# Casts and subtractions of the up projection's left forms, put in program order on their engines

## The chip, the core and the metric

One Trainium2 chip, of which the program uses one core. The metric is the device time of one execution in microseconds (us). The kernel before was run three times: 2421.71, 2421.89 and 2420.68 us, median 2421.71. All engine names are those of the profile: PE multiplies matrices, DVE, ACT and POOL work on vectors, SP issues most of the transfers.

## The reference

The program is one layer of a hybrid trunk on 1024 positions of width 1024 (three token mixers, cross-attention, a gated MLP). Only the MLP matters here. Its first half is a projection to 2 x 2816 columns, a causal convolution of width 3 over the positions, a SiLU and a product:

```
h = rms_norm(x, norm_ffn_g)
u, v = split(h @ ffn_w_up, 2)              # D_FF = 2816 each
y = silu(causal_conv3(u, ffn_conv_w, ffn_conv_b)) * v
x = x + y @ ffn_w_down
```

Everything is float32. A float32 product is made on PE from three products of rounded operands (type fp32r): an operand x is split into hi, a cast of x, and lo, the difference x - hi, and hi·hi, hi·lo and lo·hi are added up in PSUM.

## The kernel before

The up projection is `ffn_up`. It walks over 22 pairs f = 0 to 21. A pair holds 128 columns of u and 128 of v, and is done for all 1024 positions as a 2 x 2 block product with seven block products instead of eight. The right operands (T1 to T4, B11, B21, B22; 512 positions each, with hi and lo) are made once, at the end of `trunk`. The left operands, called forms here, are made afresh in every pair by the generator `left` (L1294 to L1317): A11, A12 and A22 are parts of the weights as loaded (tile `raw`), S1 to S4 are sums and differences of such parts, made on POOL (L1308). For each form `left` then issues two instructions:

- the cast (L1315) on ACT, from the part or sum into the first half of a tile `wf`,
- the subtraction (L1316) into the second half, on DVE for odd and on POOL for even numbers of a running count of forms.

`prod` (L1318 to L1324) multiplies a form with its right operand in 12 matmuls (L1323), three to each of four slices: hi·hi and hi·lo, which need the cast alone, and lo·hi, which needs the subtraction too. Where PE has done the first two matmuls of a form and not yet the third, it has started on a form whose subtraction is not there.

The tiles `wf` come from a pool with two tags of two buffers each, and the count of forms picks the tag. So the form made now takes the buffer of the form made four forms earlier, and its cast has to wait until the product of that form is done.

Pairs 0 to 5 have five forms, in program order S2, S3, S1, A22, S4: their products with B11 and B21 are done ahead of time (`ahead`, while the trunk ends) and stored. Pairs 6 to 21 have seven: A11, S2, S3, S1, A12, A22, S4. With seven forms to a pair, A11 of a pair takes the buffer of S1 of the pair before.

The products of one pair go to three places in PSUM: `ps_a` (A11 with B11, then A12 with B21), `ps_b2` (S2 with T2) and one tile of two banks, `ps_cd` (S3 with T3, S1 with T1, A22 with T4, S4 with B22). DVE reads them in turn: u2 (L1384), u3 (L1386), the upper half of vt (L1388), the lower half (L1393), the upper half of u (L1395); ACT copies `ps_a` to s1 (L1348) and u (L1391). A22 may write `ps_cd` only when vt (L1388) has been read, because waits go by whole tiles. Then y is made: L1397 (ACT), L1398 and L1399 (DVE), the SiLU L1400 (ACT), and the product with vt, L1401 (DVE).

No order is written out by hand in this function. The program is issued under a scheduler with a model of the engines' times, and that scheduler picks for every engine which of the ready instructions comes next; the streams of two or three pairs are therefore mixed on each engine. After the last pair comes `ffn_down`, whose loads of weights (tile `wdr`, L1452), sums of them (L1459, DVE) and casts (L1466, ACT) are mixed into the last pairs in the same way.

Of the kernel before, what the change touches and what calls it, by code (L numbers as in the profile page):

```python
# [12 lines left out]
F32 = mybir.dt.float32  # L13
# [4 lines left out]
ALU = mybir.AluOpType  # L18
# [78 lines left out]
class K:  # L97
# [1197 lines left out]
    def left(self, r1, r2, which, sp):  # L1295

        nc = self.nc
        V, A, G = nc.vector, nc.scalar, nc.gpsimd
        q = {f"A{n}{k + 1}": r[:, 4 * k:4 * k + 4, :] for n, r in ((1, r1), (2, r2)) if r is not None for k in range(2)}
        sums = {"S1": ("A21", "A22", ALU.add), "S2": ("S1", "A11", ALU.subtract), "S3": ("A11", "A21", ALU.subtract),  # L1300
                "S4": ("A12", "S2", ALU.subtract)}

        def get(n):
            if n not in q:
                a, b, op = sums[n]
                a, b = get(a), get(b)
                q[n] = sp.tile([P, 4, P], F32, tag=n, name=n, bufs=2 if n in ("S1", "S2") else 1)
                G.tensor_tensor(out=q[n], in0=a, in1=b, op=op)  # L1308
            return q[n]

        for n in which:
            x = get(n)
            self.nform = getattr(self, "nform", 0) + 1
            f = self.wp.tile([P, 2, 4, P], F32R, tag=("whi", "wlo")[self.nform % 2], name="wf")
            A.copy(out=f[:, 0], in_=x)  # L1315
            (V if self.nform % 2 else G).tensor_tensor(out=f[:, 1], in0=x, in1=f[:, 0].bitcast(F32), op=ALU.subtract)  # L1316
            yield f  # L1317

    def prod(self, ps, f, x, start, stop):
        n = 0  # L1320
        for k in range(4):
            for a, b in ((0, 0), (0, 1), (1, 0)):
                self.nc.tensor.matmul(ps, lhsT=f[:, a, k, :], rhs=x[b][:, k, :], start=(start and n == 0), stop=(stop and n == 11),  # L1323
                                      skip_group_check=not start)  # L1324
                n += 1
# [305 lines left out]
```

## Time and profile before

| | |
|---|---|
| median of three runs | 2421.71 us |
| the profiled execution, its own time | 2418.76 us |
| span of that execution in the profile | 2417.0 us |
| PE busy | 2312.8 us, 96% of the span |
| DVE, ACT, POOL busy | 1373.9, 908.9, 695.2 us |

The span is the time between the first and the last instruction of the profile; the execution's own time is 1.76 us longer. The times in rows are counted from the span's start. A row of the timeline has the start, the duration, the engine, the line, the operation, what it writes and reads, how many there are, and in brackets how long the engine stood idle before it and what it waited for. Matmuls overlap each other, so the pace of PE is read from one start to the next and not from the duration of one.

In the profile the up projection's end of the trunk lies at about 1728 to 1778 us, its pairs from there to about 2185 us, and the down projection behind.

### The profile page before, as it was taken

To read this page: it belongs to the slowest core of one execution; us is meant where nothing else is said; L and a number is where in the kernel's file an instruction comes from. 1 tells how busy PE (TensorE), PEld (TensorE's weight loads), DVE (VectorE), ACT (ScalarE), POOL (GpSimd) and SP (SyncE) were. 2 spreads that over 40 slices of the span, in tenths; PEclk is the share of its full clock that TensorE was granted. 3 is DMA by queue.
4 is the path that set the end of the run, shared out by engine and by line. 5 is a ranking of instruction groups with operands and counts; after the bars stand their busy time and mean duration, and the time that the engine had idled before them with its cause. 6 is when DMAs were issued, how large, how long until landed. Compare 5 with 4: busy or idle time off the path is not lost. (4 is left out here: it accounts for less than half of the span.)

```text
span 2417.0 us, 34889 instructions
## 1 busy us (share of the span) xinstructions
PE 2312.8 (96%) x13988; PEld 1887.5 (78%) x13988; DVE 1373.9 (57%) x2098; ACT 908.9 (38%) x1430; POOL 695.2 (29%) x580
## 2 busy tenths in 40 slices
PE   7999999899999999999999999999898999998998
PEld 7877768686778787888878778888676888886886
DVE  6446374757424557454564464545547656667775
ACT  6542213131314435344442233443333333334443
POOL 1011001010111333333132440141456666551041
PEclk9999999999999999999999999999999999999999
DMA  8653312121222111111103662224243322238333
GB/s 302 221 176 125 92 58 97 58 92 45 76 70 81 53 53 37 35 60 54 44 27 121 215 213 96 96 88 135 106 165 135 111 94 105 105 142 306 97 96 122
DMA packets 110930, 266.14 MB, mean 110 GB/s; under 512 B 27248, under 2 KB 31984, under 8 KB 110768
## 3 DMA queue, kind: packets, MB, share of 16 engines
q1 hardware_dynamic: 108656, 258.25, 31.9%
q0 software_dynamic: 1248, 4.46, 0.5%
q8 instruction: 110, 1.80, 0.3%
q10 hardware_dynamic: 864, 1.20, 0.1%
q14 instruction: 52, 0.43, 0.1%
HBM read 194.40 MB, written 69.47 MB: 109 GB/s over the span
## 5 line engine op out<-in xcount | busy, mean ns | idle before, releaser
L155 PE MATMUL ps_d<-hThi,whi 128*128 128x512 f32 x1056 | 425.9, 404 | 2.0 <-DVE Ktt L261 1.6
L157 PE MATMUL ps_d<-hTlo,whi 128*128 128x512 f32 x1056 | 424.2, 402 | 0.0
L159 PE MATMUL ps_d<-hThi,wlo 128*128 128x512 f32 x1056 | 424.1, 402 | 0.0
L140 ACT CAST whi<-raw 128x1024 fp32r<-128x1024 f32 (+1 forms) x170 | 167.2, 989 | 331.4 <-PE ps_d L157 155.4
L143 DVE TENSOR_TENSOR wlo<-raw,whi 128x1024 fp32r<-128x1024 f32 (+1 forms) x125 | 156.9, 1262 | 138.2 <-ACT whi L140 138.2
L155 PEld LDWEIGHTS ps_d<-hThi,whi 128*128 128x128 f32 x1056 | 199.9, 189 | 44.5 <-issue 3.2
L157 PEld LDWEIGHTS ps_d<-hTlo,whi 128*128 128x128 f32 x1056 | 199.9, 189 | 42.8 <-issue 4.6
L159 PEld LDWEIGHTS ps_d<-hThi,wlo 128*128 128x128 f32 x1056 | 199.7, 189 | 42.7 <-issue 4.2
L143 POOL TENSOR_TENSOR wlo<-raw,whi 128x1024 fp32r<-128x1024 f32 (+1 forms) x45 | 96.8, 2150 | 433.1 <-ACT whi L140 388.4
L1490 PE MATMUL ps_dn<-wd,ap 128*128 128x512 f32 x924 | 213.2, 393 | 7.1 <-ACT wd L1466 6.7
L1490 PEld LDWEIGHTS ps_dn<-wd,ap 128*128 128x128 f32 x924 | 175.1, 190 | 45.2 <-ACT wd L1466 7.1
L1315 ACT CAST wf<-S 128x512 fp32r<-128x512 f32 x88 | 54.7, 622 | 165.0 <-PE ps_cd L1323 76.5
L1466 ACT CAST ap<-acr 128x512 fp32r<-128x512 f32 x77 | 47.9, 623 | 104.2 <-PE ps_dn L1490 93.2
L1467 DVE TENSOR_TENSOR ap<-acr,ap 128x512 fp32r<-128x512 f32 x77 | 61.4, 799 | 41.4 <-ACT ap L1466 40.6
L745 DVE CUSTOM_DVE_ANT_0 a_p<-ps_s,a_bias 128x512 f32<-128x512 f32 (+3 forms) x96 | 51.7, 553 | 50.3 <-PE ps_s L743 45.0
L159 PE MATMUL ps_d<-ohi,wlo 128*128 128x512 f32 x192 | 75.9, 395 | 3.3 <-DVE wlo L143 3.3
L1316 POOL TENSOR_TENSOR wf<-S,wf 128x512 fp32r<-128x512 f32 x44 | 62.0, 1409 | 56.1 <-ACT wf L1315 56.1
L755 ACT ACTIVATE a_p<-a_p,a_nm 128x128 f32<-128x128 f32 (+7 forms) x64 | 49.2, 770 | 75.2 <-POOL a_nm L751 57.8
L157 PE MATMUL ps_d<-olo,whi 128*128 128x512 f32 x192 | 75.8, 395 | 0.0
L155 PE MATMUL ps_d<-ohi,whi 128*128 128x512 f32 x192 | 75.8, 395 | 0.0
L1113 POOL TENSOR_SCALAR ms<-ms 128x1 f32<-128x1 f32 x30 | 11.1, 371 | 224.0 <-ACT xn L1112 146.1
L1308 POOL TENSOR_TENSOR S<-raw 128x512 f32<-128x512 f32 x44 | 58.9, 1341 | 35.6 <-DVE wf L1316 21.8
(436 smaller groups left out, 5386.3 us busy)
## 6 DMA issues: line engine op xcount, KB each, us to landing
raw<-t_in SPq DMA_DIRECT2D x66, 512.0 KB, 3.6
raw<-t_up SPq DMA_DIRECT2D x50, 512.0 KB, 3.5
th_dram<-th SPq DMA_DIRECT2D x24, 512.0 KB, 2.8
mth<-th_dram SPq DMA_DIRECT2D x24, 512.0 KB, 3.7
wdr<-ffn_w_down SPq DMA_DIRECT2D x44, 256.0 KB, 5.2
acr<-act_dram SPq DMA_DIRECT2D x44, 256.0 KB, 2.7
act_dram<-y SPq DMA_DIRECT2D x20, 512.0 KB, 2.6
acr<-sums_dram SPq DMA_DIRECT2D x33, 256.0 KB, 2.6
```

The costliest lines, as they stand in the source:

```text
L140: nc.scalar.copy(out=hi, in_=raw)
L143: eng.tensor_tensor(out=lo, in0=raw, in1=hi.bitcast(F32), op=ALU.subtract)
L155: nc.tensor.matmul(o, lhsT=hi[:, k, :], rhs=xhi(k, h), start=(k == 0), stop=False)
L157: nc.tensor.matmul(o, lhsT=hi[:, k, :], rhs=xlo(k, h), start=False, stop=False)
L159: nc.tensor.matmul(o, lhsT=lo[:, k, :], rhs=xhi(k, h), start=False, stop=(k == nk - 1))
L745: V.tensor_tensor_reduce(out=p_[:, a:b], in0=ps[:, 0:b - a], in1=bias[:, 1024 - n + a:1024 - n + b], op0=ALU.add, op1=ALU.max, scale=1.0, ...
L755: A.activation(out=pr[c][:, 0:n], in_=pr[c][:, 0:n], func=AF.Exp, bias=nm[:, c:c + 1], accum_out=Z[:, c:c + 1])
L1308: G.tensor_tensor(out=q[n], in0=a, in1=b, op=op)
L1315: A.copy(out=f[:, 0], in_=x)
L1316: (V if self.nform % 2 else G).tensor_tensor(out=f[:, 1], in0=x, in1=f[:, 0].bitcast(F32), op=ALU.subtract)
L1467: V.tensor_tensor(out=t[:, 1], in0=z, in1=t[:, 0].bitcast(F32), op=ALU.subtract)
L1490: T.matmul(ps[t], lhsT=a[:, p, P * t:P * t + P], rhs=w[:, q, :], start=(not behind and j == 0 and n == 0), stop=(j == NJ - 1 and n == 2), ...
```

## The change

Each of the two instructions of a form is now issued through a helper, `inorder`. The helper keeps, for a key, the last instruction that was issued with it, and tells the scheduler that the next one of the same key has to stand behind it. There are three keys: all casts (ACT), the subtractions on DVE, and the subtractions on POOL. The sums (L1308) have none. What is computed, the buffers, the transfers and the number of instructions stay the same.

```
             f = self.wp.tile([P, 2, 4, P], F32R, tag=("whi", "wlo")[self.nform % 2], name="wf")
-            A.copy(out=f[:, 0], in_=x)
-            (V if self.nform % 2 else G).tensor_tensor(out=f[:, 1], in0=x, in1=f[:, 0].bitcast(F32), op=ALU.subtract)
+            e = self.nform % 2
+            self.inorder("A", lambda: A.copy(out=f[:, 0], in_=x))
+            self.inorder(e, lambda: (G, V)[e].tensor_tensor(out=f[:, 1], in0=x, in1=f[:, 0].bitcast(F32), op=ALU.subtract))
             yield f
+
+    def inorder(self, n, f):
+
+        last = self.__dict__.setdefault("kinds", {})
+        with self.tc.issue_after(last[n].ins) if n in last else ExitStack():
+            last[n] = f()
```

In the changed kernel the cast is L1316 and the subtraction L1317, and every later line has a number that is 7 higher (the matmul is L1330).

The scheduler's answer to the new rule shows in the order of the instructions. First ACT, from the cast of pair 8's S4 (`wf_15678`) to that of pair 9's A12 (`wf_15783`). `raw_15563` is pair 9's weight tile, `S2_15731`, `S1_15729` and `S3_15749` its sums. Before:

```order
L1315 CAST wf_15678<-S4_15676 128x512
L1315 CAST wf_15733<-S2_15731 128x512
L1400 ACTIVATE y_15547<-y_15547 128x1024
L1391 COPY u_14365<-ps_a_15567 128x512
L1315 CAST wf_15707<-raw_15563 128x512
L1315 CAST wf_15767<-S1_15729 128x512
L1315 CAST wf_15751<-S3_15749 128x512
L1348 COPY s1_15722<-ps_a_15706 128x512
L1315 CAST wf_15783<-raw_15563 128x512
```

With the change:

```order
L1316 CAST wf_15678<-S4_15676 128x512
L1407 ACTIVATE y_15547<-y_15547 128x1024
L1398 COPY u_14365<-ps_a_15567 128x512
L1316 CAST wf_15707<-raw_15563 128x512
L1316 CAST wf_15733<-S2_15731 128x512
L1316 CAST wf_15751<-S3_15749 128x512
L1355 COPY s1_15722<-ps_a_15706 128x512
L1316 CAST wf_15767<-S1_15729 128x512
L1316 CAST wf_15783<-raw_15563 128x512
```

The cast of S2 (`wf_15733`), which stood two places ahead of that of A11 (`wf_15707`), now stands behind it, and that of S1 behind that of S3.

Second PE, at the end of pair 8's product of S1 with T1 (`wf_15628`, the buffer that A11 of pair 9, `wf_15707`, takes over). Before:

```order
L1323 MATMUL ps_cd_15587<-T1lo_14151,wf_15628 128x512
L1323 MATMUL ps_cd_15587<-T1hi_14150,wf_15628 128x512
L1323 MATMUL ps_b2_15725<-T2hi_14141,wf_15733 128x512
L1323 MATMUL ps_b2_15725<-T2lo_14142,wf_15733 128x512
L1323 MATMUL ps_b2_15725<-T2hi_14141,wf_15733 128x512 x2
...
L1323 MATMUL ps_a_15706<-B11hi_13794,wf_15707 128x512
L1323 MATMUL ps_a_15706<-B11lo_13795,wf_15707 128x512
L1323 MATMUL ps_cd_15587<-T4hi_14159,wf_15660 128x512
```

With the change:

```order
L1330 MATMUL ps_cd_15587<-T1lo_14151,wf_15628 128x512
L1330 MATMUL ps_cd_15587<-T1hi_14150,wf_15628 128x512
L1330 MATMUL ps_a_15706<-B11hi_13794,wf_15707 128x512
L1330 MATMUL ps_a_15706<-B11lo_13795,wf_15707 128x512
L1330 MATMUL ps_b2_15725<-T2hi_14141,wf_15733 128x512
L1330 MATMUL ps_b2_15725<-T2lo_14142,wf_15733 128x512
L1330 MATMUL ps_cd_15587<-T4hi_14159,wf_15660 128x512
```

The twelve matmuls of pair 9's S2 (`ps_b2_15725`) stood between the end of S1 and the start of A11; now A11 follows S1 directly, and of S2 two matmuls come next and ten after A22 (`wf_15660`) and A11. At the next change of pairs S2's twelve all come after A22.

Third PE, at the change from pair 0 to pair 1. `wf_14655` is S1 and `wf_14671` A22 of pair 0; `wf_14729` is S2 and `wf_14747` S3 of pair 1. Before:

```order
L1323 MATMUL ps_cd_14614<-T1hi_14150,wf_14655 128x512
L1323 MATMUL ps_b2_14721<-T2hi_14141,wf_14729 128x512
L1323 MATMUL ps_b2_14721<-T2lo_14142,wf_14729 128x512
L1323 MATMUL ps_cd_14722<-T3hi_14291,wf_14747 128x512
L1323 MATMUL ps_cd_14722<-T3lo_14292,wf_14747 128x512
L1323 MATMUL ps_cd_14614<-T4hi_14159,wf_14671 128x512
```

With the change:

```order
L1330 MATMUL ps_cd_14614<-T1hi_14150,wf_14655 128x512
L1330 MATMUL ps_cd_14614<-T4hi_14159,wf_14671 128x512
L1330 MATMUL ps_cd_14614<-T4lo_14160,wf_14671 128x512
...
L1330 MATMUL ps_cd_14614<-T4hi_14159,wf_14671 128x512
L1330 MATMUL ps_b2_14721<-T2hi_14141,wf_14729 128x512
L1330 MATMUL ps_b2_14721<-T2lo_14142,wf_14729 128x512
```

The twelve matmuls of A22 of pair 0 moved ahead of the first matmuls of pair 1.

## Rows read from the trace of the kernel before

**Rows 1.** The page: busy us, share of the span and instructions of each engine.
```profile
PE 2312.8 (96%) x13988; PEld 1887.5 (78%) x13988; DVE 1373.9 (57%) x2098; ACT 908.9 (38%) x1430; POOL 695.2 (29%) x580
```
**Rows 2.** Windows: stretch, us; busy (instructions) of PE, PEld, DVE, ACT, POOL; clock; DMA; GB/s.
```profile
1777.90:1805.50 27.60, 21.84 (x85) 16.61 (x85) 12.74 (x16) 8.97 (x12) 18.46 (x14) 0.94 0.37 123
1805.50:1864.00 58.50, 51.98 (x216) 39.62 (x216) 38.97 (x39) 17.72 (x24) 42.77 (x29) 1.00 0.40 136
1907.83:1946.10 38.27, 38.27 (x168) 31.45 (x168) 23.93 (x26) 14.93 (x23) 24.25 (x17) 1.00 0.30 104
2156.90:2192.20 35.30, 25.03 (x108) 19.56 (x107) 23.93 (x31) 12.03 (x18) 9.34 (x8) 0.94 0.97 363
```
**Rows 3.** Timeline of PE and ACT at a change of pairs (pair 9 to 10).
```profile
1945.36 0.39 PE L1323 MATMUL ps_cd<-T1hi,wf 128*128 128x512 f32 x1
1945.58 0.39 PE L1323 MATMUL ps_b<-T2hi,wf 128*128 128x512 f32 x1
1945.78 0.62 ACT L1315 CAST wf<-raw 128x512 fp32r<-128x512 f32 x1 [0.56 <-PE ps_cd L1323]
...
1948.52 0.39 PE L1323 MATMUL ps_a<-B11hi,wf 128*128 128x512 f32 x1
```
**Rows 4.** Timeline of PE and ACT at two changes of pairs between pairs 2 and 5.
```profile
1820.90 0.39 PE L1323 MATMUL ps_cd<-T1hi,wf 128*128 128x512 f32 x1
1821.32 0.62 ACT L1315 CAST wf<-S 128x512 fp32r<-128x512 f32 x1 [1.08 <-PE ps_cd L1323]
1821.99 0.50 PE L1323 MATMUL ps_cd<-T3hi,wf 128*128 128x512 f32 x1 [0.71 <-ACT wf L1315]
1822.33 0.40 PE L1323 MATMUL ps_cd<-T3lo,wf 128*128 128x512 f32 x1
...
1837.34 0.39 PE L1323 MATMUL ps_cd<-T1hi,wf 128*128 128x512 f32 x1
1838.49 0.50 PE L1323 MATMUL ps_cd<-T3hi,wf 128*128 128x512 f32 x1 [0.76 <-ACT wf L1315]
```
**Rows 5.** PE's waits from 1805.5 to 1864 us: us in total, times, longest.
```profile
PE ps_cd L1323 <- ACT wf L1315: 3.1, 4, 0.9
```
**Rows 6.** Timeline of the end of the trunk: ACT and PE, forms made ahead.
```profile
1738.10 0.62 ACT L1315 CAST wf<-raw 128x512 fp32r<-128x512 f32 x1 [3.38 <-PE ps_a L1323]
1738.63 0.58 ACT L1257 CAST T1hi<-ps_T 128x512 fp32r<-128x512 f32 x1
1739.99 0.33 PE L1254 MATMUL ps_T<-ident,t 128*128 128x128 f32 x1 [1.09 <-DVE T1lo L1258]
```
**Rows 7.** Timeline of the change from pair 0 to pair 1: ACT, PE, DVE.
```profile
1772.74 0.63 ACT L1315 CAST wf<-raw 128x512 fp32r<-128x512 f32 x1
...
1782.68 0.39 PE L1323 MATMUL ps_cd<-T1hi,wf 128*128 128x512 f32 x1
...
1783.11 0.69 DVE L1388 TENSOR_TENSOR vt<-ps_cd,u 128x512 f32<-128x512 f32 x1 [3.19 <-PE ps_cd L1323]
...
1785.01 0.58 PE L1323 MATMUL ps_b<-T2hi,wf 128*128 128x512 f32 x1 [1.94 <-ACT wf L1315]
```
**Rows 8.** Timeline of the hand-over to the down projection: DVE and PE.
```profile
2169.14 0.69 DVE L1459 TENSOR_TENSOR wdr<-wdr 128x512 f32<-128x512 f32 x1 [5.85 <-DMA wdr<-ffn_w_down]
...
2178.59 0.47 PE L1323 MATMUL ps_cd<-T4hi,wf 128*128 128x512 f32 x1 [2.69 <-DVE vt L1388]
...
2182.45 0.47 PE L1323 MATMUL ps_cd<-B22hi,wf 128*128 128x512 f32 x1 [0.87 <-DVE vt L1393]
...
2192.14 1.22 PE L1490 MATMUL ps_dn<-wd,ap 128*128 128x512 f32 x2 [6.70 <-ACT wd L1466]
```
**Rows 9.** Timeline of DVE and POOL at the changes from pair 8 to 9 and 9 to 10.
```profile
1926.36 1.21 DVE L1401 TENSOR_TENSOR y<-y,vt 128x1024 f32<-128x1024 f32 x1
...
1944.77 1.29 POOL L1316 TENSOR_TENSOR wf<-S,wf 128x512 fp32r<-128x512 f32 x1
1944.79 2.35 DVE L1401 TENSOR_TENSOR y<-y,vt 128x1024 f32<-128x1024 f32 x1 [1.13 <-ACT y L1400]
...
1947.06 0.68 DVE L1388 TENSOR_TENSOR vt<-ps_cd,u 128x512 f32<-128x512 f32 x1
```

## The prediction

> **What bounds the kernel now.** I read the page's busy times first: PE is busy for 96% of the span, the other engines for less than 60% [rows 1]. So a change of order can cost or bring time only where PE stands still or runs at a slow clock, and the next view is the windows, by stage [rows 2]. Over two whole pairs of the steady part (7 forms each), PE is busy in 38.27 of 38.27 us: 168 matmuls, 0.228 us each, at a granted clock of 1.00, the 2.4 GHz level. Nothing can be won there; it can only be lost. PE stands idle for 5.8 us in the first two pairs (27.60 - 21.84), for 6.5 us in pairs 2 to 5 (58.50 - 51.98), and for 10.3 us at the hand-over to the down projection (35.30 - 25.03). These are all that an order of casts could win.
>
> The timeline then tells why the steady part has no gaps [rows 3]. The last matmul of pair 9's S1 starts at 1945.36. The cast of A11 of pair 10 needs the buffer that S1 frees, and starts 0.42 us later, at 1945.78. It hurts nobody, because PE goes on with S2 of pair 10 at 1945.58 and comes to A11 only at 1948.52: the twelve matmuls of S2 are the cover of this cast, and they take 2.94 us where twelve at 0.228 take 2.73.
>
> **The change, part by part.** No instruction, transfer or buffer is added or taken away. What counts is which order on PE follows from the order of the casts.
>
> *The cover at the change of pairs.* By the order of the changed kernel, PE goes from S1 of a pair straight to A11 of the next, whose cast cannot start before S1's product is done; S2's cast now stands behind A11's on ACT, so there is no other form to go on with. This holds at the changes from 7 to 8 up to 20 to 21: 14 places (at 6 to 7, A22 still lies between). The steady part has no such gap to measure, but pairs 2 to 5 have: there a cast of S3 waits in the same way for the product of S1 [rows 4]. In the first of the two the last matmul starts at 1820.90, the cast at 1821.32 (0.42 us later, as in rows 3), and the next matmul at 1821.99: 1.09 us from start to start instead of 0.228, so 0.86 us lost, and the second matmul follows after 0.34 instead of 0.228, 0.11 more: 0.97. In the second it is 1837.34 to 1838.49, 1.15, so 0.92 + 0.11 = 1.03 us. I take 0.98. That one cast is waited for and not two is because the cast of S2 starts right behind A11's and is done within the first two matmuls of A11. What the new order gives back is the 2.94 - 2.73 = 0.2 us by which S2 is stretched in every other pair, since its third matmul now comes after A22: 0.1 per change. 14 x (0.98 - 0.1) = **+12.3 us**. Bounds: 14 x 0.71 = +9.9 (the shorter idle time by itself) and 14 x 1.03 = +14.4.
>
> *The forms made ahead.* The cast at 1738.10 that stands in front of that of T1hi at 1738.63 [rows 6] is moved behind it. At most 0.53 us of PE's wait of 1.09 us for T1lo goes with that; other casts could come to stand there instead. I take **-0.3 us**, bounds -0.5 and +0.5.
>
> *Pairs 0 and 1.* After S1 of pair 0 PE waits 1.94 us for the cast of S2 of pair 1 [rows 7]. Now A22 of pair 0 is first; its cast was done at 1773.4 already. A22 must wait until DVE has read `ps_cd`: that reading starts at 1783.11 and takes 0.69, so PE goes on at about 1783.85 instead of 1785.01: -1.2 us, and S2's cast is ready when A22 is through. The load of the next raw weights is held a little longer, so I take **-1.0 us**. Low bound: -1.94, and all that the clock withholds in this stretch (granted 0.94 of 27.60 us, 1.66 us [rows 2]), together -3.6. High bound: the wait for the reading, 1783.85 - 1782.68 - 0.228 = 0.9 us, comes on top of the old one: +0.9.
>
> *Pairs 2 to 5.* PE's order stands as it was; the four waits for a cast [rows 5] stay. **0**; if POOL's sums of pairs 3 and 5, whose order differs, come late, one more wait of 0.76 in each [rows 4]: +1.5, the high bound; nothing there is made earlier, so the low bound is 0.
>
> *The hand-over.* PE's waits here are for vt (2.69 and 0.87) and for the first cast of the down projection's weights (6.70), and DVE stands 5.85 us for a load of these weights, with the work of pairs 20 and 21 behind it [rows 8]. In the new order SP has that load further back, and DVE the first of the sums behind pair 21's u3, while three more of them now stand in front of the work that PE waits for. These cancel about, by the durations (0.69 each against 5.85 that were mostly hidden behind PE's own work): **+0.5 us**. Bounds: all 10.3 us gone, or one more wait of 2.69 us.
>
> **Sum:** 12.3 - 0.3 - 1.0 + 0 + 0.5 = +11.5 us. The profiled execution took 2418.76 us, so 2430.3 on its basis. It lies 2.95 us below the median of the three runs (2421.71); on the median's basis the prediction is **2433.2 us**, 0.47% more than before. A measurement of this kernel can tell about 0.2%, 4.8 us, from no change.
>
> **The rivals.**
>
> *The hand-over pays for the gaps (not slower).* DVE's 5.85 us on the load of weights is the one large stall whose place in the order is changed. If u, u2 and vt of the last pairs, freed from it, bring the down projection's first sums and casts forward, up to 10.3 us of idle PE come back. Without the hand-over the sum is +11.0, so this decides from the point where more than 11.0 - 4.8 = 6.2 us are won; in full the sum is 11.0 - 10.3 = +0.7, 2422.4 us. For it: the load is what that stall waits for, by its row. Against it: PE's last wait, 6.70 us, is for weights that arrive while DMA is at 0.97 [rows 2], so they come no earlier by another order of DVE; the loads begin later in the new order rather than earlier. 0.14; in 0.04 of it the gaps are also smaller than priced and the kernel gets faster by over 0.2%.
>
> *A22 waits too (slower still).* In every other pair the product L1401 on DVE takes 2.35 us instead of 1.21, beside a subtraction on POOL, and vt (L1388) stands behind it: it ends at 1947.74, 2.38 us after the last S1 matmul's start [rows 9, 3]. S2's cover of 2.94 us hid that. After the change A22 comes 1.15 + 0.34 + 0.23 = 1.7 us after that start at these changes, so it would wait another 0.7 us: 7 x 0.7 = +4.9, 2438.1 us. Against it: the subtraction on POOL that lies beside L1401 is that of S2, and it moves behind A11's cast, past the end of L1401. 0.08. The Trainium skill ("SBUF — State Buffer", section "SBUF: two separate sides") calls the port pair that DVE and POOL share an exclusive lock, where whoever comes second is blocked for the whole instruction; the trace agrees (2.35 against 1.21, with 1.29 of POOL beside it), and by that rule the lengthening goes with POOL's subtraction.
>
> *The clock falls at the gaps (much slower).* After the wait of 1.94 us in pair 0 to 1 the clock was lower for a time: 0.94 over that window, 1.66 us lost. If each of the 14 new gaps had that effect, 14 x 1.66 = +23 us, 2456 us. Against it: pairs 2 to 5 have gaps of 0.7 to 0.9 us and the granted clock there is 1.00 [rows 2, 5]; those gaps are no closer together than one pair. 0.04. The Trainium skill ("TensorE: Matmul & The Clock Gate", section "A second HAM failure mode: psum-queue depth-cycling") says that frequent short idle times between groups of matmuls can make the clock go up and down, with the time of a single matmul looking right; it would make this rival's case, and the rows of pairs 2 to 5 do not bear it out.
>
> That the order does not come about at all is not a case: the order of the built program shows it.
>
> **How the numbers follow.** The forecast has 0.74, the rivals 0.14, 0.08 and 0.04. Slower by over 0.2%: 0.74 + 0.08 + 0.04 = 0.86; within 0.2%: 0.10; faster: 0.04. The forecast's own range is the sum of its nearer bounds: about 2427 to 2438 (gaps -2.4 to +2.1, pairs 0 to 1 and the trunk -2.8 to +2.7, hand-over -2 to +2, not all at one end). The range of 8 in 10 goes up to the second rival with the high bound of the gaps and some of the start, 2441, and down to 2422.5, the first rival in full; left out are the clock, the faster cases and combinations of ends.
>
> **What would show it.** Right: the window of two steady pairs is 40.0 us instead of 38.27, with PE's busy time as before and a wait of 0.7 to 0.8 us of `ps_a` for the cast at every change from 7 to 8 on, 14 of them, some 10 us in the list of waits; pair 0's wait of 1.94 us is gone and a shorter one for vt stands there; the granted clock in the steady part stays 1.00. Wrong in its size: the hand-over's idle time differs from 10.3 by more than 3 us, or `ps_cd` waits for vt in the steady part. Wrong in its mechanism: no waits of `ps_a` for the cast there, or a steady window of under 39 us.

## The result, and the profile after

The changed kernel took 2442.26 us (median of 4, 2440.16 to 2448.7) against 2421.19 us of the kernel before: 1.009, 95% interval 1.0075 to 1.0105. It is slower, as forecast, but by 21 us and not by 11.5, and 1.3 us beyond the upper end of the range. The profiled execution took 2440.16 us, 21.40 us more than that of before; the spans differ by 21.4 us too, and that is what the rows have to account for.

PE does the same work and waits longer; no other engine is busier by much. The page:

```profile
span 2438.4 us, 34897 instructions
PE 2314.7 (95%) x13988; PEld 1883.4 (77%) x13988; DVE 1370.2 (56%) x2098; ACT 906.3 (37%) x1430; POOL 708.4 (29%) x580
```

The windows of the changed kernel (columns as in [rows 2]): pairs 0 and 1, pairs 2 to 5, two pairs of the steady part, and the hand-over:

```profile
1774.00:1802.00 28.00, 21.08 (x86) 15.12 (x85) 13.90 (x15) 7.63 (x10) 17.62 (x13) 1.00 0.36 118
1802.00:1862.00 60.00, 51.27 (x214) 39.15 (x213) 36.84 (x39) 17.69 (x25) 37.02 (x27) 1.00 0.37 133
1929.10:1969.27 40.17, 38.71 (x169) 31.23 (x168) 23.32 (x26) 15.05 (x22) 26.65 (x17) 1.00 0.28 99
2174.00:2213.37 39.37, 26.90 (x108) 21.04 (x109) 24.10 (x32) 12.02 (x18) 9.86 (x8) 0.90 0.97 353
```

Two steady pairs take 40.2 us where they took 38.27 [rows 2], and PE, which was never idle there, is idle for 1.46 us. The clock stays at 1.00. The timeline at the change from pair 9 to 10, the place of [rows 3], shows the new gap:

```profile
1951.72 0.39 PE L1330 MATMUL ps_cd<-T1hi,wf 128*128 128x512 f32 x1
1952.15 0.62 ACT L1316 CAST wf<-raw 128x512 fp32r<-128x512 f32 x1 [0.32 <-PE ps_cd L1330]
1952.67 0.62 ACT L1316 CAST wf<-S 128x512 fp32r<-128x512 f32 x1
1952.82 0.50 PE L1330 MATMUL ps_a<-B11hi,wf 128*128 128x512 f32 x1 [0.71 <-ACT wf L1316]
1953.16 0.40 PE L1330 MATMUL ps_a<-B11lo,wf 128*128 128x512 f32 x1
```

The last matmul of S1 starts at 1951.72, the cast of A11 begins 0.43 us later, when S1's product has let go of the buffer, and the next matmul comes at 1952.82: 1.10 us from start to start, and the second matmul 0.34 later. That is [rows 4] once more, in a place where it did not occur before. PE's waits from 1929 to 2190 us are this one alone:

```profile
PE ps_a L1330 <- ACT wf L1316: 9.5, 13, 0.8
```

Where the 21.4 us arise is read from the starts of the first matmul of S1's product in pairs 0, 1, 5, 8 and 21, which both kernels reach with the same products done. Before, and then after the change:

```profile
1780.07 0.47 PE L1323 MATMUL ps_cd<-T1hi,wf 128*128 128x512 f32 x1 [2.17 <-DVE u L1386]
1801.72 0.39 PE L1323 MATMUL ps_cd<-T1hi,wf 128*128 128x512 f32 x1
1867.90 0.39 PE L1323 MATMUL ps_cd<-T1hi,wf 128*128 128x512 f32 x1
1923.82 0.39 PE L1323 MATMUL ps_cd<-T1hi,wf 128*128 128x512 f32 x1
2172.89 0.50 PE L1323 MATMUL ps_cd<-T1hi,wf 128*128 128x512 f32 x1
```

```profile
1777.17 0.47 PE L1330 MATMUL ps_cd<-T1hi,wf 128*128 128x512 f32 x1 [2.17 <-DVE u L1393]
1799.99 0.50 PE L1330 MATMUL ps_cd<-T1hi,wf 128*128 128x512 f32 x1 [0.26 <-DVE u L1393]
1868.51 0.39 PE L1330 MATMUL ps_cd<-T1hi,wf 128*128 128x512 f32 x1
1929.10 0.39 PE L1330 MATMUL ps_cd<-T1hi,wf 128*128 128x512 f32 x1
2190.49 0.39 PE L1330 MATMUL ps_cd<-T1hi,wf 128*128 128x512 f32 x1
2213.37 0.79 PE L1497 MATMUL ps_dn<-wd,ap 128*128 128x512 f32 x1 [6.82 <-ACT wd L1473]
```

| stretch | before | after | difference | forecast |
|---|---|---|---|---|
| start to the trunk's last matmul (L1099) | 1718.62 | 1716.02 | -2.60 | 0 |
| to S1 of pair 0 (forms made ahead) | 61.45 | 61.15 | -0.30 | -0.3 |
| S1 of pair 0 to S1 of pair 1 | 21.65 | 22.82 | +1.17 | -1.0 |
| S1 of pair 1 to S1 of pair 5 | 66.18 | 68.52 | +2.34 | 0 |
| S1 of pair 5 to S1 of pair 8 | 55.92 | 60.59 | +4.67 | +0.9 |
| S1 of pair 8 to S1 of pair 21 (13 changes) | 249.07 | 261.39 | +12.32 | +11.4 |
| S1 of pair 21 to the down projection | 19.25 | 22.88 | +3.63 | +0.5 |
| down projection to the end | 224.86 | 225.03 | +0.17 | 0 |

The first line is not of the change: the trunk's last matmul comes at 1714.38 and 1718.62 us in the two profiles whose start is that of before, and at 1714.21 to 1720.52 in eight with the rule at the start. (The two kernels with five buffers throughout, below, are apart from that.) The other lines are single readings too. S1 of pair 0 to S1 of pair 1 takes 21.65 and 22.39 us in the two profiles with the old order, and 22.22 to 24.00 in six that have the full change's order there; the second profile of the full change has 70.1 for pairs 1 to 5 and 62.2 for pairs 5 to 8. Only the line of the 13 changes repeats closely, 261.39 to 261.49 in three profiles.

### The profile page after: what moved, and what is told of

Same layout as the page of the kernel before. It is cut to its first block, busy times and chain, and to the rows that moved or that the text cites. A ratio compares the mean times of both kernels' runs of the same rounds, so it can differ in the third digit from the quotient of the medians.

```text
span 2438.4 us, 34897 instructions
## 1 busy us (share of the span) xinstructions
PE 2314.7 (95%) x13988; PEld 1883.4 (77%) x13988; DVE 1370.2 (56%) x2098; ACT 906.3 (37%) x1430; POOL 708.4 (29%) x580
## 5 line engine op out<-in xcount | busy, mean ns | idle before, releaser
L1316 ACT CAST wf<-S 128x512 fp32r<-128x512 f32 x88 | 53.7, 620 | 114.7 <-PE ps_cd L1330 72.0
L1317 POOL TENSOR_TENSOR wf<-S,wf 128x512 fp32r<-128x512 f32 x44 | 67.6, 1537 | 72.6 <-ACT wf L1316 72.4
L1330 PE MATMUL ps_a<-B11hi,wf 128*128 128x512 f32 x176 | 61.5, 411 | 14.2 <-ACT wf L1316 12.2
```

Source lines behind the costliest of these rows:

```text
L1316: self.inorder("A", lambda: A.copy(out=f[:, 0], in_=x))
L1317: self.inorder(e, lambda: (G, V)[e].tensor_tensor(out=f[:, 1], in0=x, in1=f[:, 0].bitcast(F32), op=ALU.subtract))
```

## The experiments

**What the rule is made of.** The rule has three keys, and the built programs answer one question without a run: with the keys for the subtractions alone, the order on all five engines is that of the kernel before; with the key for the casts alone it is that of the full change, instruction by instruction. All that follows is about the casts.

The first four runs split the change by pairs, and take away the cause that I supposed. Before was at 2418.6 us on that chip.

**The start alone.** A form's number is counted through the program; 42 are made up to pair 5.

```
-        with self.tc.issue_after(last[n].ins) if n in last else ExitStack():
+        with self.tc.issue_after(last[n].ins) if n in last and self.nform <= 42 else ExitStack():
```

> The rule holds for the forms made ahead and for pairs 0 to 5 alone; the order of PE from pair 6 on is that of the kernel before. Theory (the loss is in the gaps after S1 from pair 7 to 8 on, in the two pairs ahead of these, and in the hand-over): only what the start does is left. By the two profiles the trunk's end came 2.9 us earlier and pairs 1 to 5 lost 3.5 us of that, so +0.6 us or, if the earlier trunk is chance and not of the change, +3.5 us: 2422 to 2425 us, no waits of ps_a for a cast after pair 8. Rival (the early part shifts everything behind it and the rest of the loss follows from that shift): well above +5 us.

Measured: 2422.09 us, 1.0012 (1.0003 to 1.0021), +2.9 us by the ratio. The pairs from 6 on run as before (S1 of pair 8 to S1 of pair 21: 248.95 us). The rival falls; the start costs some 3 us, and the trunk's earlier end does not count.

**Everything but the start.** The same line with `self.nform > 42`.

> The rule holds from pair 6 on alone; the start is that of the kernel before. Theory: 1.8 us between pairs 5 and 6, 0.2 at 6 to 7, 2.7 at 7 to 8, 12.3 over the other 13 changes of pairs, 3.6 at the hand-over, +20.6 us, 2442 us: as slow as the full change. Rival (the start carries part of the loss): 3 us or more faster than the full change, 2439 us or less.

Measured: 2439.41 us, 1.0090 (1.0075 to 1.0104), +21.8 us. The pieces in its trace are those of the full change (pair 5 to 8: 60.5 us, 8 to 21: 261.5, hand-over 22.7). So the two halves add up, 2.9 + 21.8 = 24.7 us, against 21.8 and 27.1 for the full change by the ratios of its two measurements. The figure of 2439 for the rival was reached, but on a chip where before was 2.6 us faster; by the ratio it is not.

**Pairs 20 and 21 free.** The same line with `self.nform <= 42 + 7 * 14`.

> The rule holds for the forms made ahead and for pairs 0 to 19; pairs 20 and 21 are free, and PE's order there is that of the kernel before. Theory (the hand-over's 3.6 us come from where the sums of the down projection's weights stand on DVE in front of vt of pair 21): two gaps of 0.95 and the 3.6 us are gone, 5.5 us less than the full change, 2437 us, and PE's wait for vt of pair 21 is 2.7 us instead of 4.8. Rival (the hand-over is late because of when the loads come, whatever the order): two gaps less only, 2440 us, and the wait for vt stays above 4 us.

Measured: 2437.85 us, 1.0081 (1.0068 to 1.0095), +19.6 us. The full change gave 21.8 by its first measurement and 27.1 by its second, so the time alone does not part the two theories. The trace decides: PE's waits in the hand-over, from 2160 to 2212 us, are those of before.

```profile
PE ps_dn L1497 <- ACT wd L1473: 6.7, 1, 6.7
PE ps_cd L1330 <- DVE vt L1395: 2.7, 1, 2.7
PE ps_cd L1330 <- DVE vt L1400: 0.9, 1, 0.9
```

In the full change the wait for vt of pair 21 is 4.77 us, and DVE's rows tell why:

```profile
2191.96 0.69 DVE L1466 TENSOR_TENSOR wdr<-wdr 128x512 f32<-128x512 f32 x1 [2.32 <-DMA wdr<-ffn_w_down]
2192.57 1.28 DVE L1406 SCALAR_TENSOR_TENSOR y<-u,par,y 128x1024 f32<-128x1024 f32 x1
2193.77 1.89 DVE L1466 TENSOR_TENSOR wdr<-wdr 128x512 f32<-128x512 f32 x3
...
2197.31 0.68 DVE L1395 TENSOR_TENSOR vt<-ps_cd,u 128x512 f32<-128x512 f32 x1
...
2198.14 0.47 PE L1330 MATMUL ps_cd<-T4hi,wf 128*128 128x512 f32 x1 [4.77 <-DVE vt L1395]
```

The wait for the load of weights did move behind u3, but the next link of pair 20's chain, L1406, is behind it now, then three more sums, the SiLU and L1408, and vt last. That is 2.1 of the 3.6 us. The rest goes with the clock: in eight profiles with the same 2.7 us wait the hand-over took 19.25 us (before, granted clock 0.89 over it) to 21.74 (the start alone, 0.77), 20.5 in the mean; in the three with the wait of 4.7 to 4.8 us it took 22.68 to 22.88 (0.82 to 0.83). So the change costs some 2.3 us here, and the other 1.3 are there because the profiled run of before was one of the two fastest at this place.

**A12 ahead of S1.** In pairs 6 to 21 A12 is made and multiplied before S1, so that A11 of the next pair takes A12's buffer.

```
-                forms = self.left(*rs, ... else ("A11", "S2", "S3", "S1", "A12", "A22", "S4"), sp)
+                forms = self.left(*rs, ... else ("A11", "S2", "S3", "A12", "S1", "A22", "S4"), sp)
...
-                self.prod(d, next(forms), X["T1"], True, True)
-                V.tensor_tensor(out=vt[:, 512:1024], in0=d, in1=u3, op=ALU.add)
                 if f >= ne:
                     self.prod(a, next(forms), X["B21"], False, True)
                     A.copy(out=u[:, 2:514], in_=a)
+                self.prod(d, next(forms), X["T1"], True, True)
+                V.tensor_tensor(out=vt[:, 512:1024], in0=d, in1=u3, op=ALU.add)
```

> The full change, and in pairs 6 to 21 the form A12 is made and multiplied ahead of S1, so that the form that takes S1's buffer in the next pair is S2 and not A11; A11 takes that of A12, whose product is done 2.7 us earlier. Theory (the gap is the wait of A11's cast for the buffer of S1): no wait of ps_a for a cast in the steady part, 19.04 us to a pair, 12.3 us of gaps and most of the 2.7 us at 7 to 8 gone, 2427 to 2430 us with the hand-over as in the full change. Rival (the gaps come from casts that follow each other on ACT in a fixed order, whatever the buffer): a wait of 0.7 us at each change stays, 2440 us or more.

Measured: 2431.22 us, 1.0055 (1.0041 to 1.0068). The waits for a cast are gone from the steady part, with the casts still in a fixed order: the buffer is the cause. The time is above the forecast because another wait stands there instead, from 1930 to 2150 us:

```profile
PE ps_cd L1330 <- DVE u L1393: 3.1, 5, 0.6
```

S1 comes later in the pair, and at every second change PE now waits for DVE to read the shared PSUM tile; two pairs take 39.3 us, halfway between 38.3 and 40.2. At the change to pair 21 one wait for u3 is 3.57 us long, and the wait for vt behind it is 0.88 instead of 4.77: the stall of the hand-over has moved ahead of S1. From S1 of pair 8 to S1 of pair 21 it takes 259.0 us all the same, so of the 12.3 us lost there the swap brings only 2.4 back. It shows where the wait for the cast comes from, and not that the time can be had.

The next four ran beside before at 2418.5 us.

**A11 left out of the rule.**

```
-            self.inorder("A", lambda: A.copy(out=f[:, 0], in_=x))
+            if n == "A11" and len(which) == 7:
+                A.copy(out=f[:, 0], in_=x)
+            else:
+                self.inorder("A", lambda: A.copy(out=f[:, 0], in_=x))
```

> The full change, but the cast of A11 of pairs 6 to 21 is left out of the rule; all other casts stay in program order. PE's order from pair 7 on becomes that of the kernel before. Theory (the one cast that waits for S1's buffer holds those behind it on ACT, and that is the loss from pair 7 on): no wait of ps_a for a cast in the steady part, a pair in 19.15 us, wait for vt of pair 21 2.7 us; what stays is 3.2 us of pairs 0 to 5 and about 1 us at 5 to 6, so +4 to +6 us, 2423 to 2426 us. Rival (the other casts' order counts as well): more than +10 us.

Measured: 2426.95 us, 1.0038 (1.0024 to 1.0051), +9.2 us: less than the full change by more than half, more than the theory had. One cast of seven is freed, and pair 8 to 21 takes 252.29 us instead of 261.39, pairs 5 to 8 57.0 instead of 60.6, the hand-over 19.25 instead of 22.88 (2.1 us of that by the wait for vt, which is 2.7 again). What is left in the steady part, 252.29 - 249.07 = 3.2 us, does not stand in the list of PE's waits; the weight loads wait for subtractions of S2 and of A12, on POOL above all (PEld, 1930 to 2150 us; in the kernel before the same list has 2.0 us for POOL at S2 and nothing at A12), and why POOL is later there I did not follow:

```profile
L1333 PEld LDWEIGHTS ps_b<-T2hi,wf 128*128 128x128 f32 x96 | 17.1, 188 | 6.8 <-POOL wf L1320 2.4 <-DVE wf L1320 1.4
...
L1333 PEld LDWEIGHTS ps_a<-B21hi,wf 128*128 128x128 f32 x89 | 16.2, 188 | 6.4 <-POOL wf L1320 3.2
```

**S4 left out of the rule, start alone.** The same edit with `n == "S4"`, on the kernel with the start alone.

> The rule for the forms made ahead and pairs 0 to 5 as in the run before of that kind, but the casts of S4 are left out of it, so that they can go ahead of A22's again. Theory (in pairs 1 to 5 the loss is a chain: S4's cast behind A22's, which waits for a buffer, S4's subtraction late, POOL's sum for the next S4 late, and S2's subtraction behind that sum): PE's waits for a subtraction of S2 in pairs 2 to 5 fall back to 0.5 to 0.6 each, and the median comes down by some 2 us against that run, to +0.5 to +1.5 us. Rival (the loss is the changed order of POOL's sums or the S3 and S1 casts): the waits stay at 0.9 to 1.5, +3 us.

Measured: 2421.48 us, 1.0010 (1.0000 to 1.0021), about as with the rule for S4. Four waits for a subtraction lie between S1 of pair 1 and S1 of pair 5, those of S2 of pairs 3 to 5 and of A11 of pair 6. Of 1.10, 0.91, 1.55 and 0.91 us the first fell back to 0.63 and the third to 1.16, and the other two stayed (0.90 and 0.91). The chain that I had drawn is at most half of it; what the waits may have in common is POOL's sum for the next S4, tested below.

**Five buffers.** The same edit on the kernel before and on the full change:

```
-            f = self.wp.tile([P, 2, 4, P], F32R, tag=("whi", "wlo")[self.nform % 2], name="wf")
+            b = self.nform % 5
+            f = (sp if b == 4 else self.wp).tile([P, 2, 4, P], F32R, tag=("whi", "wlo", "whi", "wlo", "wx")[b], name="wf", bufs=1 if b == 4 else 2)
...
-    ctx.enter_context(tc.tile_pool(name="top", bufs=1, side="right")).tile([P, 16], F32, name="top")
+    ctx.enter_context(tc.tile_pool(name="top", bufs=1, side="right")).tile([P, 8], F32, name="top")
```

> The kernel before with a fifth buffer for the forms (room for it comes from an unused tile). Theory (casts that wait for the buffer of S1 or S4 cost 0.7 to 1 us each in pairs 1 to 5, where nothing lies between): those waits vanish, some 8 to 9 us less, 2410 to 2413 us, and the steady part has nothing to give (19.04 against 19.15 us a pair, 1.5 us). Rival (another tie takes the place of the buffer, the tile of PSUM that S1, S3, A22 and S4 share, or the sums on POOL): no change, 2418 us or more.

> The full change with the fifth buffer. Theory (a fixed order of casts costs only where a cast waits for a buffer of a product that PE has just done): A11's cast no longer waits for S1, so no waits of ps_a for a cast in the steady part, and with the waits of pairs 1 to 5 gone too the kernel is as fast as the one before with five buffers, within 3 us. Rival: waits for casts at each change of pairs stay, 2430 us or more.

Measured: 2444.46 us, 1.0103 (1.0090 to 1.0116), and 2450.04 us, 1.0128 (1.0115 to 1.0141). Both are slower than the kernel before. Ten us of each arise ahead of the up projection (the trunk's last matmul at 1728.8 and 1728.3): the unused tile that was cut from 64 to 32 bytes a partition lies under others, and in the built program their places have moved by 32 bytes, while PE's order up to the first form is the same. The 8000th recorded matmul outside the forms, in the middle of the trunk, is at 1085.0 and 1086.3 us already, where the twelve other profiles have 1073.5 to 1077.0. Why that costs time is open. So the two runs do not tell what a fifth buffer alone is worth. In the up projection the wait did not go away in the kernel in order, it went for the greater part to the next form, since with five buffers S2 takes that of S1, and PE had done A11 already (1930 to 2150 us; two waits of `ps_a`, 1.2 us, are left):

```profile
PE ps_b L1331 <- ACT wf L1317: 5.1, 7, 0.8
```

In free order the scheduler mixes the pairs in another way with each number of buffers, and S1 of pair 8 to S1 of pair 21 takes 259.26 us, for 1080 matmuls where the kernel before has 1092, with few waits of matmuls listed. Why is open.

The four that follow ran beside before at 2419.1 and, the last of them, 2417.8 us.

**The sum for S4 behind S2's subtraction, start alone.**

```
+                with self.tc.issue_after(subs["S2"].ins) if n == "S4" else ExitStack():
                     G.tensor_tensor(out=q[n], in0=a, in1=b, op=op)
...
+            subs[n] = self.kinds[e]
             yield f
```

> The rule for the forms made ahead and pairs 0 to 5, and besides POOL's sum for S4 of a pair has to stand behind the subtraction of S2 of that pair. Theory (what is left of the loss in pairs 2 to 5 is that sum, ahead of S2's subtraction on POOL where POOL makes it, beside it on SBUF where DVE makes it): PE's waits for a subtraction in pairs 2 to 5 are 0.5 to 0.65 each as before the change, and from S1 of pair 1 to S1 of pair 5 pass 66 us instead of 68.5. Rival (the sum is not what delays it): waits of 0.9 or more stay.

Measured: 2416.66 us, 0.9995 (0.9986 to 1.0005): no slower than before, where the start alone had +2.9 us. (The sum is moved in all pairs, so 1.1 us of that come from pairs 8 to 21, 247.86 us against 248.95.) With the start alone, at the change to pair 5, the rows were (POOL, PE):

```profile
1846.36 1.28 POOL L1308 TENSOR_TENSOR S<-raw,S 128x512 f32<-128x512 f32 x1 [0.63 <-DVE wf L1317]
...
1847.60 1.27 POOL L1317 TENSOR_TENSOR wf<-S,wf 128x512 fp32r<-128x512 f32 x1
...
1848.92 0.72 PE L1330 MATMUL ps_b<-T2hi,wf 128*128 128x512 f32 x2 [1.55 <-POOL wf L1317]
```

and with the sum moved they are:

```profile
1848.43 1.28 POOL L1319 TENSOR_TENSOR wf<-S,wf 128x512 fp32r<-128x512 f32 x1 [1.31 <-ACT wf L1318]
...
1849.67 1.29 POOL L1309 TENSOR_TENSOR S<-raw,S 128x512 f32<-128x512 f32 x1
1849.77 0.73 PE L1333 MATMUL ps_b<-T2hi,wf 128*128 128x512 f32 x2 [0.63 <-POOL wf L1319]
```

The waits are 0.63 and 0.63 where POOL makes the subtraction and none where DVE does; S1 of pair 1 to S1 of pair 5 takes 65.7 us (66 expected). So the 2.3 us of this stretch are POOL's sum. In the steady part, which the rule for casts does not touch here, each stretch from one S1 to the next, from pair 7 to pair 20, now takes 19.04 us (the last one, to pair 21, 19.38).

**Five buffers for pairs 0 to 5 alone, free order.** On the kernel before:

```
-            f = self.wp.tile([P, 2, 4, P], F32R, tag=("whi", "wlo")[self.nform % 2], name="wf")
+            b = self.nform % 5 if len(which) == 5 else self.nform % 2
+            f = (sp if b == 4 else self.wp).tile([P, 2, 4, P], F32R, tag=("whi", "wlo", "whi", "wlo", "wx")[b], name="wf", bufs=1 if b == 4 else 2)
...
-                s1 = sp.tile([P, 512], F32, tag="s1", name=nm, bufs=3)
+                s1 = sp.tile([P, 512], F32, tag="s1", name=nm, bufs=2)
...
-                    s1 = sp.tile([P, 512], F32, tag="s1", name="s1", bufs=3)
+                    s1 = sp.tile([P, 512], F32, tag="s1", name="s1", bufs=2)
```

> The kernel before, free order, with a fifth buffer for the forms of pairs 0 to 5 alone (room for it from the third buffer of s1, which no other pool's place depends on). PE's order from pair 6 on is that of the kernel before; in pairs 1 to 5, S3 of the next pair comes ahead of S1. Theory (a cast that waits for a product just done costs 0.7 to 1 us, wherever it stands): the waits of S3 and most of those of S2 for a cast in pairs 1 to 5 vanish, 5 to 9 us less than the kernel before. Rival (the PSUM tile that a pair's products share takes the place of the buffer, waits for vt or u3): less than 3 us.

Measured: 2413.71 us, 0.9979 (0.9970 to 0.9989): 5.1 us less than the kernel before, the low end of what was expected. In its profile S1 of pair 0 to S1 of pair 5 is 2.8 us shorter than before, and where the rest comes from is not shown. PE's longest waits from 1788 to 1865 us:

```profile
PE ps_cd L1324 <- DVE vt L1389: 5.7, 4, 2.4
PE ps_b L1324 <- ACT wf L1316: 2.2, 3, 0.8
```

All waits of `ps_cd` for a cast, 3.1 us in [rows 5], are gone. The rival holds for a part: with S3 ahead of S1, A22 comes sooner after S1 and waits for vt.

**The full change again.**

> The full change once more, beside the kernel before on this chip. All theories: 18 to 24 us slower, 13 waits of ps_a for a cast of 0.7 us in the steady part, a wait of 4.8 us for vt of pair 21; a trunk end that comes 2 us or more after that of the run before it would show that the 2.6 us there are chance.

Measured: 2444.08 us, 1.0112 (1.0096 to 1.0128); 2440.37 us in its profiled run, with the waits of pairs 2 to 21 in the same places. The trunk's last matmul is at 1715.6, so the sign of chance that was named did not come; that the earlier trunk is chance rests on the kernels with the old start, above. Two stretches are longer than in the first profile with the same waits: S1 of pair 3 to S1 of pair 4 takes 18.82 us instead of 17.49, and S1 of pair 7 to S1 of pair 8 23.76 instead of 22.19. The granted clock is 0.92 and 0.93 over them, where it was 1.00: behind waits of 1.49 and 1.24 us PE goes on at 0.43 us a matmul, the 1.2 GHz level, for some 3 us.

**Both improvements together.** The edits of the run with five buffers for pairs 0 to 5 and of the run with the sum moved, on the kernel before.

> The kernel before in free order, with both changes that each helped by itself: a fifth buffer for the forms of pairs 0 to 5, and POOL's sum for S4 of a pair behind the subtraction of S2 of that pair (all pairs). Theory (the two work at different places, the first in pairs 1 to 5, the second in the steady part, 1.2 us over 13 pairs as in the run with that sum moved): about 1 to 1.5 us less than the run with the fifth buffer alone, 0.997 to 0.998 of the kernel before, a steady pair in 19.04 us. Rival (the sum moved behind makes S4 late where pairs 1 to 5 run closer together): no better than the fifth buffer alone.

Measured: 2414.54 us, 0.9984 (0.9973 to 0.9994). S1 of pair 8 to S1 of pair 21 takes 247.72 us, 1.2 less than with the fifth buffer alone (248.92), so the sum's effect is there; but S1 of pair 1 to S1 of pair 2 takes 19.6 us where it took 17.4. Of these 2.1 us, 0.56 are a longer wait for vt (2.93 instead of 2.37): DVE's L1404 (the product with vt) there runs beside POOL's subtraction and takes 2.36 us instead of 1.22. The rest goes with the clock, 0.91 over that stretch against 1.00. The two kernels are the same within their intervals; that the sum makes S4 late, as the rival has it, is not shown.

## Why the prediction was right or wrong

**The sign and the main term held.** The cover at the change of pairs is what is lost. The forecast said 0.98 us a gap less 0.1 for S2, 14 times, +12.3 us. Measured from pair 8 to 21 are 12.32 us in 13 gaps, 0.95 each (forecast 0.88), with 0.7 to 0.8 us of listed wait, the granted clock at 1.00, and 40.2 us for two pairs (40.0 forecast). The price was taken from a stretch where the same wait already stood [rows 4], and that price was good. That the buffer of S1 is the cause is shown by A12 ahead of S1 and by A11 left out of the rule: each takes the wait away in its own manner.

**The step that failed is the treatment of the places outside the steady part as cancelling.** The sum had -0.3 - 1.0 + 0 + 0.5 = -0.8 us there; the trace, without the trunk's chance, has -0.3 + 1.2 + 2.3 + 4.7 + 3.6, and without the one gap, at 7 to 8, that belongs to the main term, that is about +10.6. Of the two signs that the text gave for a wrong size, the idle time of the hand-over stays within its 3 us (12.5 against 10.3), and a wait of `ps_cd` for vt shows once, at the first of the 14 changes. Most of the loss arose where no sign had been set. Term by term:

- *Pairs 0 and 1*, forecast -1.0. A22 did wait only 0.88 us for vt (0.9 forecast), and the wait of 1.94 us [rows 7] went. But new waits came behind it: 0.43 for S2's cast and 1.10 for S3's subtraction in pair 1, and 1.28 for S2's cast in pair 2 where 0.71 stood, with 0.79 for its subtraction:

```profile
1781.04 0.47 PE L1330 MATMUL ps_cd<-T4hi,wf 128*128 128x512 f32 x1 [0.88 <-DVE vt L1395]
...
1784.44 0.50 PE L1330 MATMUL ps_b<-T2hi,wf 128*128 128x512 f32 x1 [0.43 <-ACT wf L1316]
...
1786.81 0.73 PE L1330 MATMUL ps_cd<-T3hi,wf 128*128 128x512 f32 x2 [1.10 <-DVE wf L1317]
...
1795.64 0.50 PE L1330 MATMUL ps_b<-T2hi,wf 128*128 128x512 f32 x1 [1.28 <-ACT wf L1316]
...
1797.16 0.73 PE L1330 MATMUL ps_b<-T2hi,wf 128*128 128x512 f32 x2 [0.79 <-DVE wf L1317]
```

  The step priced the wait that went and only the first that came. No run takes these waits away one by one, so this is read from the rows alone; and with 21.65 and 22.39 us for the old order in two profiles, the +1.2 is known to about 1 us.
- *Pairs 2 to 5*, forecast 0 because PE's order stands. PE's order did stand, and the time of the forms did not: POOL's sum for S4, put ahead of S2's subtraction, cost 2.3 us. The text named POOL's sums and allowed 1.5 us for them as the far bound. It had looked at one line [rows 5] of the list of PE's waits; the lines that grew stand further down in it, the waits for a subtraction. Before, and then after (1802 to 1862 us):

```profile
PE ps_b L1323 <- POOL wf L1316: 1.3, 2, 0.6
PE ps_b L1323 <- DVE wf L1316: 0.5, 1, 0.5
```

```profile
PE ps_b L1330 <- POOL wf L1317: 2.6, 2, 1.5
PE ps_b L1330 <- DVE wf L1317: 0.9, 1, 0.9
```

  An unchanged order on the engine that bounds says nothing of its waits.
- *Pairs 5 to 8*, forecast one gap. The gap at 5 to 6 was overlooked (before, S3's twelve matmuls of pair 6 lie between). At 6 to 7 a gap stood before already, A11's wait for its cast; now A22 follows S1 and waits for vt instead, 0.88 us as in pair 0. Before, and then after:

```profile
1890.58 0.50 PE L1323 MATMUL ps_a<-B11hi,wf 128*128 128x512 f32 x1 [0.75 <-ACT wf L1315]
```

```profile
1872.16 0.50 PE L1330 MATMUL ps_b<-T2hi,wf 128*128 128x512 f32 x1 [0.76 <-ACT wf L1316]
...
1890.51 0.47 PE L1330 MATMUL ps_cd<-T4hi,wf 128*128 128x512 f32 x1 [0.88 <-DVE vt L1395]
```

  S1 of pair 6 waits another 0.53 us for u3. At 7 to 8 two waits follow each other: A11's for its cast is 1.33 us, longer than the gap of the main term, since the SiLU and the copy of u stand in front of that cast on ACT (it starts at 1910.45), and A22 waits 1.24 us for vt. There the second rival did happen, which the forecast had for the steady part. The rows show the long product that it named, 2.33 us on DVE, though beside a sum on POOL and not the subtraction:

```profile
1910.10 1.26 POOL L1308 TENSOR_TENSOR S<-raw,S 128x512 f32<-128x512 f32 x1
1910.11 2.33 DVE L1408 TENSOR_TENSOR y<-y,vt 128x1024 f32<-128x1024 f32 x1 [1.13 <-ACT y L1407]
...
1911.12 0.50 PE L1330 MATMUL ps_a<-B11hi,wf 128*128 128x512 f32 x1 [1.33 <-ACT wf L1316]
...
1912.37 0.68 DVE L1395 TENSOR_TENSOR vt<-ps_cd,u 128x512 f32<-128x512 f32 x1
...
1913.10 0.50 PE L1330 MATMUL ps_cd<-T4hi,wf 128*128 128x512 f32 x1 [1.24 <-DVE vt L1395]
```

  The Trainium skill ("SBUF — State Buffer", section "SBUF: two separate sides") speaks of an exclusive lock on the port that DVE and POOL share; the row agrees, 2.33 us against 1.21 for the same product [rows 9]. Later it did not happen: from S1 of pair 8 on the product L1408 took 1.22 to 1.23 us, 13 times. S2's subtraction had moved past it, as was said against the rival; but at the change from 9 to 10 a sum on POOL ends at 1951.42 where L1408 starts at 1951.39, so that no sum lies beside it there is luck.
- *The hand-over*, forecast +0.5 on the ground that the moves cancel. The three sums that the text saw in front of pair 21's work, with L1406 behind the load, were not hidden: 2.1 us, as the run with pairs 20 and 21 free shows. The other 1.5 go with the clock, which differs there from run to run; over all profiles the change costs some 2.3 us here.

**The rivals.** The hand-over did not pay for anything; it became slower. The clock did not fall at the gaps of the main term: 1.00 from pair 8 on in both profiles of the full change. The ground given was thin, though: in pairs 2 to 5 of the kernel before PE waits ten times and not four, so the gaps there are closer together than one pair, still at 1.00. And ahead of pair 8 the clock did fall in the second profile of the full change, which cost about 2.9 us there. The range ended at 2441, the second rival with the high bound of the gaps and some of the start; its room was meant for waits in the steady part. That the measured time lies so near its end is luck: pairs 2 to 5 passed their own high bound (+1.5), the hand-over came near its own (+2.7) or passed it, and pairs 5 to 8 had none beyond one gap.

## What to carry to other kernels

A scheduler's free order can hide a wait for a buffer behind another product, and a rule that puts instructions in program order takes that cover away: before fixing an order, look which instruction waits for a buffer that the bounding engine has just used, and what is queued behind it on its engine. When a rule moves one engine's instructions, the other engines' queues move as well; price each queue that feeds the bounding engine, also where that engine's own order stays. In the kernel before, one more buffer, only in the stretch where nothing covers the wait, brought 0.9979 of the time.

## What was not expected of the hardware

With the unused tile cut by 32 bytes a partition, to make room for a fifth buffer for all pairs, some 10 us were lost ahead of the up projection (the trunk's last matmul at 1728.8 and 1728.3 us), and a cause was not looked for. The trunk's end differs by 6 us between the other profiled runs (1714.2 to 1720.5) with no change to it, more than several of the terms of the sum. The same wait may or may not be followed by a slow stretch: behind 1.24 us for vt at 7 to 8 the granted clock over S1 of pair 7 to S1 of pair 8 was 1.00 in one profile of the full change and 0.93 in the other, 1.6 us apart.

One thing is of the scheduler and not of the chip. Which buffer a form takes depends on the order that it finds: the built programs show A11 on that of S1 of the pair before from pair 7 on, as told ahead of the prediction, but in pairs 2 to 5 S2 waits for S4 of two pairs back, not for the form four earlier in program order, which is why a wait for a cast stands at S2 there too.
